# Two token groups through both layers of a two-layer decoder trunk, the second group's first mixer spread over the first group's whole way

## The chip, the cores and the metric

The kernel is one program on one NeuronCore of a Trainium2 chip. Its metric is the device time of one execution in microseconds (us), the median of three runs. The core has five engines with their own instruction streams: TensorE (PE, matrix products; its weight loads are shown as PEld), VectorE (DVE), ScalarE (ACT), GpSimd (POOL) and SyncE (SP), which here issues nearly all DMA transfers. They wait for one another by semaphores. Each engine carries out its instructions in the order in which they were written, so an instruction that waits holds up all that stand behind it on its engine. Matmuls accumulate in PSUM, eight banks of 512 float32 per partition; all else is in SBUF or in HBM, the chip's main memory.

## What is computed

One step of a decoder with two layers and a model width of 1024, for 1024 prompt tokens and 8 x 8 sample tokens, 1088 columns in all:

```python
for layer in range(2):
    hn = rms_norm(h, norm_mix_g[layer])
    if layer == 0:     # conformer convolution beside stick-breaking attention
        a_val, a_gate, q, k, v = split(hn @ w_in_even)              # 5 x 512
        a = silu(layer_norm(causal_conv31(a_val * sigmoid(a_gate))))
        b = stick_breaking_attention(q, k, v)   # sample tokens: paged past K and V too
        mix = concat(a, b) @ w_out_even
    else:              # short gated convolution beside causal pooling
        gb, gc, xv, u = split(hn @ w_in_odd)                        # 4 x 512
        c = gb * causal_conv3(gc * xv)
        d = per_group_linear(trailing_mean(u) - u) * pool_scale     # windows 2, 4, 8, 16
        mix = concat(c, d) @ w_out_odd
    h = h + mix
    g, u = split(rms_norm(h, norm_ffn_g[layer]) @ w_ffn_in[layer])  # 2 x 2816
    h = h + (silu(g) * u) @ w_ffn_out[layer]
y = rms_norm(h, norm_final_g)
```

Everything is float32. New keys, values and convolution and pooling states are returned beside `y`.

## The kernel before

Activations lie transposed, channels on the partitions and tokens in the columns: `hb` holds the residual in 8 chunks of 128 channels by 1088 columns. A float32 product is made of three: weights and activations are each split into a high part and a rest (`hl` and `x1`), and `mm3` adds high x high, high x rest and rest x high. A weight tile of 512 KB (8 slices of 128 x 128) is loaded by SP into `stage`, copied by ScalarE (L152) and subtracted by GpSimd (L153) into `hl`. Both have three buffers; `w_next` hands out one tile and starts the split two ahead. The order of the tiles is the list `seq`.

Columns are worked in groups. `GA` is the first 512 prompt tokens, one matmul of 512 columns per slice and product. `GB` is the other 512 and the 64 sample tokens, two matmuls of 288. `GT` is all 1088, in 364, 364 and 360. Weights of layer 0 are therefore read and split twice, those of layer 1 once.

The stages in order: input projection of A (0 to 157 us), of B (to 349.6), output projection and channel mixer of A (to 1096.6), the same of B (to 1576.9), then layer 1 for all columns (to 2656), and the last output blocks with the final norm.

`run_in` makes an input projection of 128 output channels per tile; its first two tiles run slice by slice together (`pair`), so that the norm of the input (`norm_hooks`) can be made meanwhile. `run_out` makes an output projection, which begins and ends with a pair. `run_ffn` makes the channel mixer: for every two of its 22 hidden chunks four input tiles (`one`), then the output blocks of the two chunks before (`out_block`, six matmuls of A each, evicted by `added`, L230). A chunk's product and its split into `hid` are put on the list `post` and written when `flush` is next called. Every matrix result is evicted by VectorE, scaled (L226) or added (L230). `prep` makes a next operand, high part on ScalarE (L304), rest on VectorE (L307). `mix_operand` splits a mixer's result into `x1` and reloads the residual from `park` in HBM.

Work with little matrix content runs between the matmuls as a generator. `bg` writes its next piece; `slot` is a place where that is called, after every two slices of a tile, after each tile and each output block. While A does its output projection and channel mixer of layer 0, the flow is: attention of B (scores L801, sigmoids L806, scans L815 and L818, product L820, transposes L830, values L839), then the convolution of B (L693) with the attention of the sample tokens (page transposes L928, scores L951, weight transposes L1000, values L1012), then the norm after the convolution. `drain` writes what is left at once.

In layer 1 `ev_u` and `ev_xv` evict, and put on `post` the window sums (`f2`, then `f3` with the pooling matmuls, L1348) and the gated product on GpSimd with the short convolution (L1271, L1281, L1292). At the end `to_y` works the last output blocks in 24 items of 384 columns or fewer, transposes each (L1402), multiplies by the gain and, per 384 tokens, scales by the norm and stores.

Of the kernel before, what the change touches and what calls it, by code (L numbers as in the profile page):

```python
# [16 lines left out]
D = 1024  # L17
# [29 lines left out]
GT = Grp(0, T, 364)  # L47
# [11 lines left out]
def trunk_kernel(ctx, tc, x_prompt, x_sample, cache_k, cache_v, state_conformer, state_shortconv, state_pool,  # L59
# [14 lines left out]
    tmpbox = [gstack.enter_context(tc.tile_pool(name="tmpg", bufs=4, side="right")), 640]  # L74

    def tmp():
        return tmpbox[0].tile([128, tmpbox[1]], F, name="tmp")
# [42 lines left out]
    for _ in range(2):  # L120
        for j, c in EVEN:
            add_in(w_in_even[0], 512 * j + c * 128)
    for _ in range(2):
        for n in range(8):
            add_in(w_out_even[0], n * 128)
        add_ffn(0)

    ODD = [(j, c) for c in range(4) for j in (3, 1, 2, 0)]
# [104 lines left out]

    def flush():
        todo = post[:]
        post.clear()
        for f in todo:
            f()
# [41 lines left out]
    def run_in(g, accs, x, evacs, hooks, ks=K0, tail=(lambda: None,) * 2):  # L280
        a0, a1 = pair(g, accs, x, K0, hooks)
        evacs[0](a0)
        evacs[1](a1)
        for i, e in enumerate(evacs[2:]):
            h = w_next()
            a = accs()
            end = i == len(evacs) - 3
            block(g, a, h, x, ks if end else K0, flush)
# [3 lines left out]
            if end:  # L292
                tail[1]()
        flush()
# [57 lines left out]
    def run_ffn(g, accs, ps, hidp, x, last, sig=False, slot=lambda: None):  # L352
# [16 lines left out]
        def ev_u(f, a):  # L369
# [7 lines left out]
            def fin():  # L377
                pool.tensor_tensor(t[:, :n], t[:, :n], u[:, :n], op=OP.mult)  # L378
                split(dst, t[:, :n])
# [10 lines left out]
        for q in range(G + 1):  # L390
            if q < G:
                for f in (2 * q, 2 * q + 1):
                    if f == 0:
                        run_in(g, accs, x, [ev_g, lambda a: ev_u(0, a)], norm_hooks(g, ps))
# [4 lines left out]
            if q == G:  # L399
                flush()  # L400
# [214 lines left out]
    def ev_k(g, hp):  # L615
        def f(a):
            scaled(g, kall[:, hp, g.cs], a)
            post.append(lambda: rows_out(g, kall[:, hp, g.cs], k_p, k_s, hp))
        return f

    def ev_v(g, hp):
        def f(a):
            t = tmp()
            scaled(g, t[:, :g.n], a)
            post.append(lambda: rows_out(g, t, v_p, v_s, hp))
# [130 lines left out]
    def attention(g):  # L756
# [3 lines left out]
        with ExitStack() as es_:  # L760
# [11 lines left out]
            def operands(h):  # L772
# [7 lines left out]
                for c in range(0, NKEY, 512):  # L780
                    small.append(lambda c=c: dve.tensor_tensor(k[o, c:c + 512], ks[:, c:c + 512],
                                                               f32(k[r, c:c + 512]), op=OP.subtract))
                small.append(lambda: act.activation(q[o], qs, AF.Copy))
                small.append(lambda: dve.tensor_tensor(qz[hh][r], qs, f32(q[r]), op=OP.subtract))
# [297 lines left out]
    def in_proj(g, x, first, slot):  # L1082
# [21 lines left out]
        flush()  # L1104

# [44 lines left out]

    acc_pool(GA, 3)
    hstack = ExitStack()
    hidp = hstack.enter_context(tc.tile_pool(name="hid0", bufs=2, side="right"))
# [39 lines left out]
    hstack.close()  # L1193


    acc_pool(GB, 3)
    run_out(GB, accs, x1, FFNG)
    tstack, r1stack = ExitStack(), ExitStack()
    sq = list(range(KC))

    def slot_d():
        turn[0] += 1
        if sq and turn[0] % 4 == 0:
            n = sq.pop(0)
            add_squares(GA, hb[:, n, GA.cs], n == 0)

    def to_mixer(hh):
        nonlocal x1
        assert not sq
        x1stack.close()  # L1210
        gstack.close()
        tmpbox[:] = [tstack.enter_context(tc.tile_pool(name="tmps", bufs=3, side="right")), 1152]
        r1p = r1stack.enter_context(tc.tile_pool(name="r1", bufs=1, side="right"))
        x1 = [r1p.tile([128, 2, T], FR, name=f"x1t_{c}") for c in range(KC)]
        for o in range(2):
            h = w_next()
            for i in range(4):
# [257 lines left out]
```

## Time and profile before

| | us |
|---|---|
| median of 3 runs (2706.16 to 2709.74) | 2708.54 |
| the profiled execution's own time | 2708.54 |
| its span, first to last instruction | 2706.8 |
| TensorE busy | 2603.3 |
| VectorE busy | 1212.3 |
| GpSimd busy | 1031.1 |
| ScalarE busy | 868.3 |

In a row of the timeline stand start, duration, engine, line, operation, tile written and read, shape and count, and in brackets the idle time of the engine before it with what ended it. In a row of groups the count is followed by busy time, mean ns of one, and idle time before them. In a row of windows stand the window, its length, the busy time of PE, PEld, DVE, ACT and POOL, the granted TensorE clock, the busy share of the DMA engines and GB/s. Matmuls overlap; their rate is read from start to start.

### The profile page before, as it was taken

How to read it: one execution, taken by the hardware profiler on the slowest of the kernel's cores; microseconds unless marked ns; L12 is line 12 of the kernel's file. 1: busy time of each engine (PE TensorE's matmuls, PEld its weight loads, DVE VectorE, ACT ScalarE, POOL GpSimd, SP SyncE). 2: the span in 40 equal slices, each digit the busy share in tenths (PEclk: the TensorE clock that was granted, in tenths of full speed). 3: DMA queues.
4: the chain of work that ended last, by engine and by line, in shares of the span. 5: the costliest groups of instructions: out<-in, count | busy, mean ns of one | idle time of the engine just before them, and what ended most of it. 6: DMA issues, size and time to landing. Idle time of an engine off the chain costs nothing. (4 is left out here: it accounts for less than half of the span.)

```text
span 2706.8 us, 37823 instructions
## 1 busy us (share of the span) xinstructions
PE 2603.3 (96%) x15423; PEld 2365.3 (87%) x15423; DVE 1212.3 (45%) x1730; ACT 868.3 (32%) x1326; POOL 1031.1 (38%) x589
## 2 busy tenths in 40 slices
PE   8989998998999998999999989999999999999997
PEld 6788876887666656899999989999999999999997
DVE  4774776868677642322222243343122222222226
ACT  4436765653433323332222232132211111111112
POOL 5655243343333337464444442224222222222222
PEclk9999999999999999999999999999999999999999
DMA  6432231234444432422222221131111111111111
GB/s 198 123 96 78 66 99 40 62 90 133 144 137 146 120 110 70 136 86 86 79 86 87 79 91 47 43 106 47 39 48 39 47 47 40 48 47 40 47 39 67
DMA packets 293380, 218.75 MB, mean 81 GB/s; under 512 B 21505, under 2 KB 248961, under 8 KB 293192
## 3 DMA queue, kind: packets, MB, share of 16 engines
q1 hardware_dynamic: 293176, 216.33, 26.8%
q8 instruction: 122, 2.00, 0.3%
q14 instruction: 50, 0.41, 0.1%
q10 hardware_dynamic: 32, 0.01, 0.0%
HBM read 198.09 MB, written 18.69 MB: 80 GB/s over the span
## 5 line engine op out<-in xcount | busy, mean ns | idle before, releaser
L153 POOL TENSOR_TENSOR hl<-stage,hl 128x1024 fp32r<-128x1024 f32 x278 | 679.5, 2446 | 1209.9 <-ACT hl L152 816.6
L170 PE MATMUL acc<-x1t,hl 128*128 128x364 f32 (+1 forms) x4896 | 824.1, 330 | 7.1 <-DVE hb L230 6.5
L170 PEld LDWEIGHTS acc<-x1t,hl 128*128 128x128 f32 x4896 | 817.2, 189 | 9.2 <-ACT x1t L304 6.7
L170 PE MATMUL acc<-x,hl 128*128 128x288 f32 (+1 forms) x4704 | 804.3, 325 | 12.9 <-DVE hb L230 9.6
L170 PEld LDWEIGHTS acc<-x,hl 128*128 128x128 f32 x4704 | 690.8, 189 | 88.7 <-issue 39.6
L170 PE MATMUL acc<-hid,hl 128*128 128x364 f32 (+2 forms) x3024 | 530.4, 333 | 20.5 <-DVE hb L230 17.5
L170 PEld LDWEIGHTS acc<-hid,hl 128*128 128x128 f32 x3024 | 480.0, 190 | 58.4 <-DVE hb L230 23.2
L152 ACT ACTIVATE hl<-stage 128x1024 fp32r<-128x1024 f32 x278 | 292.1, 1054 | 585.9 <-PE acc L170 318.5
L226 DVE TENSOR_TENSOR tmp<-acc,rr 128x728 f32<-128x728 f32 (+2 forms) x230 | 160.6, 720 | 684.3 <-PE acc L170 681.6
L230 DVE TENSOR_TENSOR hb<-acc,hb 128x728 f32<-128x728 f32 (+2 forms) x368 | 255.3, 720 | 273.2 <-PE acc L170 272.2
L176 DVE TENSOR_TENSOR hid<-tmp,hid 128x512 fp32r<-128x512 f32 (+2 forms) x66 | 60.8, 921 | 201.8 <-ACT hid L175 201.6
L187 POOL TENSOR_TENSOR ss<-ss,tmp 128x512 f32<-128x512 f32 (+2 forms) x55 | 98.4, 1789 | 91.6 <-ACT tmp L186 89.3
L378 POOL TENSOR_TENSOR tmp<-tmp 128x512 f32<-128x512 f32 (+2 forms) x66 | 117.1, 1774 | 29.3 <-ACT tmp L366 28.2
L175 ACT ACTIVATE hid<-tmp 128x512 fp32r<-128x512 f32 (+2 forms) x66 | 53.4, 809 | 230.8 <-POOL tmp L378 230.8
L170 PE MATMUL acc<-x1a,hl 128*128 128x512 f32 x480 | 122.4, 408 | 3.7 <-POOL hl L153 2.3
L366 ACT ACTIVATE tmp<-tmp 128x576 f32<-128x576 f32 (+1 forms) x44 | 39.6, 900 | 256.1 <-DVE tmp L226 256.1
L170 PEld LDWEIGHTS acc<-x1a,hl 128*128 128x128 f32 x480 | 89.9, 191 | 27.1 <-POOL hl L153 3.8
L693 DVE SCALAR_TENSOR_TENSOR cacc<-ext,par,cacc 128x512 f32<-128x512 f32 x120 | 90.1, 751 | 2.3
L364 POOL TENSOR_TENSOR tmp<-tmp 128x512 f32<-128x512 f32 x22 | 31.7, 1439 | 120.3 <-ACT tmp L363 113.1
L839 PE MATMUL o<-wt,vrow 128*64 128x128 f32 x576 | 76.6, 278 | 0.4 <-ACT wt L831 0.4
L818 DVE TENSOR_TENSOR_SCAN q<-q,ones 128x384 f32<-128x384 f32 (+6 forms) x56 | 76.0, 1357 | 2.0
L655 DVE SCALAR_TENSOR_TENSOR cacc<-ext,par,cacc 128x512 f32<-128x512 f32 x100 | 75.4, 754 | 3.0
(222 smaller groups left out, 1880.2 us busy)
## 6 DMA issues: line engine op xcount, KB each, us to landing
stage<-in_w_ffn_in_dram SPq DMA_DIRECT2D x132, 512.0 KB
stage<-in_w_ffn_out_dram SPq DMA_DIRECT2D x66, 512.0 KB
stage<-in_w_in_even_dram SPq DMA_DIRECT2D x40, 512.0 KB
kst<-in_cache_k_dram SPq DMA_DIRECT2D x64, 256.0 KB
vst<-in_cache_v_dram SPq DMA_DIRECT2D x64, 256.0 KB
stage<-in_w_out_even_dram SPq DMA_DIRECT2D x16, 512.0 KB
stage<-in_w_in_odd_dram SPq DMA_DIRECT2D x16, 512.0 KB
park<-hb SPq DMA_DIRECT2D x16, 288.0 KB
```

Source lines behind the costliest of these rows:

```text
L152: act.activation(hl[:, 0], st, AF.Copy)
L153: pool.tensor_tensor(hl[:, 1], st, f32(hl[:, 0]), op=OP.subtract)
L170: pe.matmul(acc[:, b, :c1 - c0], w, x[:, xi, c0:c1], start=first and s == 0, stop=last and s == 2)
L176: dve.tensor_tensor(dst[:, 1], src, f32(dst[:, 0]), op=OP.subtract)
L187: pool.tensor_tensor(ss[:, g.cs], ss[:, g.cs], t[:, :g.n], op=OP.add)
L226: dve.tensor_tensor(d, a, r, op=OP.mult)
L230: dve.tensor_tensor(d, a, d, op=OP.add)
L378: pool.tensor_tensor(t[:, :n], t[:, :n], u[:, :n], op=OP.mult)
L655: dve.scalar_tensor_tensor(acc, i, w, acc, op0=OP.mult, op1=OP.add)
L693: dve.scalar_tensor_tensor(o, i, w, o, op0=OP.mult, op1=OP.add)
L818: dve.tensor_tensor_scan(e, e, ones[:, 0:1].to_broadcast([128, n - 128]), q[:, n - 128:n - 127], op0=OP.mult, op1=OP.mult)
L839: pe.matmul(o, vrow[h][:, j], w[:, j], start=j == 0, stop=j == i)
```

## The change

There is no group of all columns any more. A goes through layer 0 and layer 1 to its last residual; then B does. The weights of layer 1 are read and split once for each. The flow of B's layer 0 mixer is the same, but is called in every second slot (`bg2`) of A's way from the first output projection to the last channel mixer, whose slots now include those of `run_in`. A's layer 1 hands the last 15 pooling inputs and the last 2 convolution inputs to B (`uhalo`, `ghalo`). The first 512 rows of `y` are made and stored by a new flow, `flow_y`, in slots of B's output projection and channel mixer of layer 0; the end works 16 items, of 256 and 320 columns.

Smaller edits: the rest of a hidden chunk's split goes on a second list, `late`, written one `flush` later; the row copies of keys and values (`rows_out`) are written one `flush` later; the rests of the attention's keys and queries are subtracted by GpSimd instead of VectorE. `tmp` keeps 4 buffers of 640 columns throughout, where layer 1 had 3 of 1152.

```diff
     for _ in range(2):
         for n in range(8):
             add_in(w_out_even[0], n * 128)
         add_ffn(0)
-    for j, c in ODD:
-        add_in(w_in_odd[0], j * 512 + c * 128)
-    for n in range(8):
-        add_in(w_out_odd[0], n * 128)
-    add_ffn(1)
+        for j, c in ODD:
+            add_in(w_in_odd[0], j * 512 + c * 128)
+        for n in range(8):
+            add_in(w_out_odd[0], n * 128)
+        add_ffn(1)
...
+    late = []
+
     def flush():
-        todo = post[:]
+        todo, low_parts = post[:], late[:]
         post.clear()
-        for f in todo:
+        late.clear()
+        for f in todo + low_parts:
             f()
...
-    def run_in(g, accs, x, evacs, hooks, ks=K0, tail=(lambda: None,) * 2):
-        a0, a1 = pair(g, accs, x, K0, hooks)
+    def run_in(g, accs, x, evacs, hooks, ks=K0, tail=(lambda: None,) * 2, slot=lambda: None):
+        a0, a1 = pair(g, accs, x, K0, hooks, slot)
...
             def fin():
                 pool.tensor_tensor(t[:, :n], t[:, :n], u[:, :n], op=OP.mult)
-                split(dst, t[:, :n])
+                act.activation(dst[:, 0], t[:, :n], AF.Copy)
+                late.append(lambda: dve.tensor_tensor(dst[:, 1], t[:, :n], f32(dst[:, 0]), op=OP.subtract))
...
             if q == G:
+                flush()
                 flush()
                 last(hid.pop(q - 1))
...
-            post.append(lambda: rows_out(g, kall[:, hp, g.cs], k_p, k_s, hp))
+            post.append(lambda: post.append(lambda: rows_out(g, kall[:, hp, g.cs], k_p, k_s, hp)))
...
-                    small.append(lambda c=c: dve.tensor_tensor(k[o, c:c + 512], ks[:, c:c + 512],
-                                                               f32(k[r, c:c + 512]), op=OP.subtract))
+                    small.append(lambda c=c: pool.tensor_tensor(k[o, c:c + 512], ks[:, c:c + 512],
+                                                                f32(k[r, c:c + 512]), op=OP.subtract))
...
+    def to_mixer(g, slot):
+        def f(hh):
+            for o in range(2):
+                h = w_next()
+                for i in range(4):
+                    n = o * 4 + i
+                    a = accs()
+                    out_block(g, a, h, i, hh)
+                    added(g, hb[:, n, g.cs], a)
+                    sp.dma_start(park[:, n, g.cs], hb[:, n, g.cs])
+                    prep(g, x1, n, pc(MIXG + 8 + n), squares=True)
+                    low(1)
+                    slot()
+            low()
+        return f
+
+    def mixer1(g, slot):
+        own = g is GA
...
+                    def f2():
+                        pool.tensor_tensor(q[:, :g.n], q[:, :g.n], t[:, :g.n], op=OP.mult)
+                        ext = mx.tile([128, 2 + NX], F, name="ext1")
+                        act.activation(ext[:, 2:514], q[:, 0:512], AF.Copy)
...
+                        if own:
+                            pool.memset(ext[:, 0:2], 0.0)
+                            act.activation(ghalo[:, c], q[:, 510:512], AF.Copy)
+                        else:
...
+                            pe.transpose(m[:66, 0:128], q[:, 510:576], ident)
+                            act.activation(rowc[:66, c * 128:c * 128 + 128], m[:66, 0:128], AF.Copy)
...
+            evs = [(ev_gb, ev_gc, ev_xv, ev_u)[j](c) for j, c in ODD]
+            run_in(g, accs, x1, evs, norm_hooks(g, ms), ks=KS, slot=slot,
+                   tail=(lambda: mix_operand(g, x1, KS[:1]), lambda: mix_operand(g, x1, KS[1:7])))
+            mix_operand(g, x1, KS[-1:])
...
+    turn[0] = 0
+
+    def bg2():
+        turn[0] += 1
+        if turn[0] % 2:
+            bg()
+
     mix_operand(GA, x1, K0)
-
-    run_out(GA, accs, x1, FFNG, slot=bg)
+    run_out(GA, accs, x1, FFNG, slot=bg2)
+    ffn(GA, to_mixer(GA, bg2), True, bg2)
+    mixer1(GA, bg2)
+    run_out(GA, accs, x1, FFNG + 8, KS, slot=bg2)
 
     def last_a(hh):
         drain()
...
                 out_block(GA, a, h, i, hh)
                 mix_operand(GB, x1, [n])
                 added(GA, hb[:, n, GA.cs], a)
-                sp.dma_start(park[:, n, GA.cs], hb[:, n, GA.cs])
-
-    run_ffn(GA, accs, ms, hidp, x1, last_a, sig=True, slot=bg)
+                add_squares(GA, hb[:, n, GA.cs], n == 0)
+
+    ffn(GA, last_a, True, bg2)
 
     acc_pool(GB, 3)
-    run_out(GB, accs, x1, FFNG)
...
+    def flow_y():
+        with tc.tile_pool(name="ya", bufs=1) as yp:
...
+            norm_cols(ms, D, 0, 4)
+            yield 1
+            for n in range(8):
+                m = ms()
+                for t in range(4):
+                    pe.transpose(m[:, t * 128:t * 128 + 128], hb[:, n, t * 128:t * 128 + 128], ident)
+                dve.tensor_tensor(y[:, :, n * 128:n * 128 + 128], m.rearrange("p (t c) -> p t c", t=4),
+                                  gall[:, None, n * 128:n * 128 + 128].to_broadcast([128, 4, 128]), op=OP.mult)
+                yield 1
+            for t in range(4):
+                act.activation(y[:, t], y[:, t], AF.Copy, scale=rstd[:, t:t + 1])
+                sp.dma_start(y_p[0, t * 128:t * 128 + 128], y[:, t])
+                yield 1
+
+    flow.append(flow_y())
+    run_out(GB, accs, x1, FFNG, slot=bg2)
+    ffn(GB, to_mixer(GB, lambda: None), False, bg2)
+    drain()
+    mixer1(GB, lambda: None)
+    run_out(GB, accs, x1, FFNG + 8, KS)
...
+    YB = ((0, 256), (256, 576))
...
-        for q in range(24 + LAG):
-            if q < 24:
+        for q in range(16 + LAG):
+            if q < 16:
                 item(q)
...
+    ffn(GB, to_y, False, lambda: None)
```

More of the change, by code (lines that the diff above doesn't have):

```diff
@@ L122, in trunk_kernel @@
             add_in(w_in_even[0], 512 * j + c * 128)
+    ODD = [(j, c) for c in range(4) for j in (3, 1, 2, 0)]
     for _ in range(2):
@@ L287, in run_in @@
             end = i == len(evacs) - 3
-            block(g, a, h, x, ks if end else K0, flush)
+            block(g, a, h, x, ks if end else K0, flush, slot)
             if end:
@@ L1104, in in_proj @@
         flush()
+        flush()
     phase = {}
```

353 lines of the change are left out of this document (164 added, 189 removed).

## The prediction

> **What bounds the kernel now.** I read the page first, then busy time by stage, then TensorE's waits, then the timeline at the longest of them.
>
> ```profile
> span 2706.8 us, 37823 instructions
> PE 2603.3 (96%) x15423; PEld 2365.3 (87%) x15423; DVE 1212.3 (45%) x1730; ACT 868.3 (32%) x1326; POOL 1031.1 (38%) x589
> ```
>
> The span is 2706.8 us, and TensorE is without work for 2706.8 - 2603.3 = 103.5 us of it. The profiled execution's own time is 2708.54 us, 1.74 us above its span; it is also the median of the three runs. By stage (length, TensorE's busy time, the other engines', the granted clock):
>
> ```profile
> 0.00:157.00 157.00, 138.97 (x611) 107.44 (x612) 97.91 (x149) 73.31 (x106) 94.92 (x63) 0.99 0.52 153
> 157.00:349.60 192.60, 184.73 (x1323) 170.69 (x1321) 116.84 (x171) 111.89 (x224) 86.97 (x82) 0.98 0.27 76
> 349.60:1096.60 747.00, 694.60 (x3257) 512.64 (x3257) 505.83 (x736) 334.35 (x589) 291.16 (x180) 0.97 0.36 108
> 1096.60:1576.90 480.30, 472.04 (x3567) 470.66 (x3567) 142.09 (x184) 135.31 (x161) 237.78 (x115) 1.00 0.30 89
> 1576.90:2656.00 1079.10, 1077.12 (x6436) 1070.09 (x6436) 315.80 (x408) 195.86 (x217) 302.87 (x133) 1.00 0.16 48
> 2656.00:2706.80 50.80, 35.84 (x235) 33.75 (x234) 33.84 (x85) 17.59 (x31) 17.35 (x18) 0.90 0.24 89
> ```
>
> Layer 1 (1576.9 to 2656) is idle for 2.0 us in 1079: only its matmuls count there. Half of all idle time, 747.0 - 694.6 = 52.4 us, lies where group A does layer 0's output projection and channel mixer with the flow of group B's mixer between its matmuls. TensorE's waits in that stretch (total, times, longest):
>
> ```profile
> PE acc L170 <- DVE hb L230: 26.9, 8, 7.4
> PE m L1000 <- ACT wts L1001: 9.5, 4, 3.7
> PE m L830 <- DVE be L820: 7.5, 5, 3.5
> ```
>
> **The matmuls themselves.** Layer 1 has 16 + 8 + 44 + 22 = 90 weight tiles of 24 (slice, product) steps each. A step was three matmuls of 364, 364 and 360 columns; it becomes one of 512 in A and two of 288 in B.
>
> ```profile
> 1042.51 15.64 PE L170 MATMUL acc<-x,hl 128*128 128x512 f32 x66
> 1057.98 0.40 PE L170 MATMUL acc<-hid,hl 128*128 128x512 f32 x1
> ...
> 1215.80 24.49 PE L170 MATMUL acc<-x,hl 128*128 128x288 f32 x184
> ...
> 2007.99 42.32 PE L170 MATMUL acc<-x1t,hl 128*128 128x364 f32 x253
> ```
>
> (1057.98 - 1042.51)/66 = 234.4 ns, 24.49/184 = 133.1 ns, 42.32/253 = 167.3 ns. Old step 501.9 ns, new 234.4 + 266.2 = 500.6 ns: 2160 x -1.3 = **-3 us**. So two passes over layer 1 cost TensorE nothing.
>
> The splits of a weight tile, by the groups of instructions:
>
> ```profile
> L153 POOL TENSOR_TENSOR hl<-stage,hl 128x1024 fp32r<-128x1024 f32 x278 | 679.5, 2446 | 1209.9 <-ACT hl L152 816.6
> L152 ACT ACTIVATE hl<-stage 128x1024 fp32r<-128x1024 f32 x278 | 292.1, 1054 | 585.9 <-PE acc L170 318.5
> ```
>
> The 90 further weight tiles are 90 x (1.05 us on ScalarE and 2.45 us on GpSimd), under the 5.6 us that A's 24 matmuls take per tile.
>
> **What half the rate removes.** A piece of flow went into every turn, now into every second. By the code the flow has 73 + 180 + 31 = 284 pieces (attention, sample with convolution, norm), so it needs 567 turns; group A now has 31 + 256 + 8 + 63 + 31 + 256 = 645, and the flow ends inside its second channel mixer. VectorE, busy 505.8 of 747 us, gets about (747 + 2160 x 0.234)/747 = 1.7 times the time for the same pieces. Of the 26.9 us, 7.4 is one stop at 446 us and 9.5 lies in A's last output blocks (both below); the other 10 with 9.5 + 7.5 make 27 us of waits on the flow. I leave 8 (6 of them L1000's, whose nine transposes stand in one piece with two PSUM buffers, so its wait is its own): **-19**; bounds -27 and -5. The fill's deferred low part (`late`) belongs here: VectorE no longer stands before it.
>
> Long waits also cost clock (windows again, the third figure from the end):
>
> ```profile
> 446.00:449.00 3.00, 3.00 (x7) 2.36 (x8) 2.29 (x3) 2.98 (x5) 2.41 (x2) 0.50 0.56 163
> 1576.90:1580.00 3.10, 3.10 (x10) 3.10 (x11) 2.94 (x2) 1.70 (x2) 2.94 (x3) 0.50 1.03 374
> ```
>
> After the waits that end at 445.9 and 1576.9 us the granted clock is 0.50. The stretch's mean of 0.97 is 22 us of withheld clock in 747, about half of it while matmuls ran: 11 us, of which I take **-6** with the waits. [...]
>
> **The stop at 446 us**, in the timeline:
>
> ```profile
> 439.41 5.09 POOL L153 TENSOR_TENSOR hl<-stage,hl 128x1024 fp32r<-128x1024 f32 x2 [0.86 <-ACT hl L152]
> 439.50 5.55 DVE L781 TENSOR_TENSOR kt<-kall,kt 64x512 fp32r<-64x512 f32 x2
> ...
> 445.91 1.19 PE L170 MATMUL acc<-x,hl 128*128 128x512 f32 x2 [7.38 <-DVE hb L230]
> ```
>
> From the output projection's closing pair to the channel mixer's opening pair, three weight buffers allow one prefetch, so the second tile is split only after the closing pair: 1.05 + 2.45 = 3.5 us whatever else happens. The rest was VectorE, held by two key subtractions (L781) ahead of the evictions; these go to GpSimd. 7.4 becomes about 3.9: **-3.5** (bounds -4 and 0). The same transition comes once more, in layer 1: **+4.5** with its clock. [...]
>
> **Group A's last blocks** (1058 to 1096.6). The stretch by its windows:
>
> ```profile
> 1030.00:1096.60 66.60, 54.19 (x220) 41.38 (x218) 26.52 (x40) 26.51 (x35) 40.86 (x24) 0.94 0.35 108
> ```
>
> and, in the timeline,
>
> ```profile
> 1072.58 0.63 ACT L175 ACTIVATE hid<-tmp 128x512 fp32r<-128x512 f32 x1 [5.89 <-POOL tmp L378]
> 1073.24 0.69 DVE L176 TENSOR_TENSOR hid<-tmp,hid 128x512 fp32r<-128x512 f32 x1 [8.77 <-ACT hid L175]
> 1074.59 10.70 PE L170 MATMUL acc<-hid,hl 128*128 128x512 f32 x36 [5.68 <-DVE hb L230]
> ...
> 1096.59 3.67 PE L170 MATMUL acc<-x,hl 128*128 128x288 f32 x26 [2.23 <-DVE hb L230]
> ```
>
> TensorE idles 12.4 us here, 9.5 of them for L230 (5.7, 2.2 and two below 1). The evictions stood behind L176, which waited for ScalarE, which waited for GpSimd still at the flow's norm. With `late` and a flow that has ended, 5.7 and some 2 of the rest go; the new squares and their GpSimd sums give about 2.5 back: **-5** (bounds -10 and +3).
>
> **The passage into layer 1.** In the timeline:
>
> ```profile
> 1576.88 5.36 PE L170 MATMUL acc<-x1t,hl 128*128 128x364 f32 x20 [6.46 <-DVE hb L230]
> ```
>
> and VectorE's groups kept apart by shape, the first of the stretch 1555 to 1577, the others of the whole span:
>
> ```profile
> L307 DVE SCALAR_TENSOR_TENSOR x1t<-hb,par,x1t 128x1088 fp32r<-128x1088 f32 x7 | 13.3, 1906 | 0.3 <-ACT x1t L304 0.3
> ...
> L230 DVE TENSOR_TENSOR hb<-acc,hb 128x576 f32<-128x576 f32 x96 | 71.4, 755 | 78.8 <-PE acc L170 78.3
> L307 DVE SCALAR_TENSOR_TENSOR x<-hb,par,x 128x576 fp32r<-128x576 f32 x16 | 21.1, 1332 | 6.0 <-ACT x L304 6.0
> L230 DVE TENSOR_TENSOR hb<-acc,hb 128x512 f32<-128x512 f32 x96 | 64.7, 684 | 20.5 <-PE acc L170 20.3
> L307 DVE SCALAR_TENSOR_TENSOR x<-hb,par,x 128x512 fp32r<-128x512 f32 x8 | 9.5, 1204 | 4.9 <-ACT x L304 4.9
> ```
>
> VectorE took 0.76 + 1.91 us per output block of 12 x 0.133 = 1.6 us, and the new PSUM pool waited: 6.46, and 3.1 - 10 x 0.167 = 1.4 for the clock. Now B needs 0.76 + 1.33 = 2.1 against 1.6, eight times 0.5 less the slack of the accumulators: 3. **-5**. Group A pays newly: 0.68 + 1.20 = 1.9 against 6 x 0.234 = 1.4, so **+4**.
>
> **Layer 1's token mixer, in halves.** In the gate block GpSimd multiplies, and a transpose of the product stands in the middle of that block on TensorE (from the chain of waits):
>
> ```profile
> 1773.81 1.07 ACT hl L152
> 1774.88 0.07 issue
> 1774.95 2.41 POOL hl L153
> 1777.35 2.50 POOL tmp L1271
> ...
> 1779.91 0.30 PE m L1281
> ```
>
> The chain from the block's start (1773.8) to the transpose takes 6.1 us and fits just in half a block of 72 x 0.167 / 2 = 6.0 us. In B half a block is 24 x 0.133 = 3.2 us; the chain keeps its first 3.5 us and multiplies 576 columns.
>
> ```profile
> L578 POOL TENSOR_TENSOR hb<-tmp 128x576 f32<-128x576 f32 x4 | 5.8, 1460 | 6.0 <-ACT tmp L576 6.0
> ```
>
> 1.1 + 2.4 + 1.5 = 5.0 against 3.2: 1.7 us of stop, four times, **+7**, with the 2 us of old waits gone **+5** (bounds 0 and +10). A has no such transpose, but the pooling matmuls behind VectorE's window sums come 5.6 us later instead of 12: **+2.5**, and 2 for the reload of the residual and the last low part (bounds 0 and +12 together). B's second passage from pair to pair waits as its first did:
>
> ```profile
> 1150.45 2.77 PE L170 MATMUL acc<-x,hl 128*128 128x288 f32 x19 [1.53 <-POOL hl L153]
> ```
>
> **+1.5**; and the low part deferred past the last block is late by some 0.5 us in four places, **+2**. In the input projections the row copies leave one flush later: **-1.5**, since the long stop at their end stays (it waits for an eviction behind the convolution). The first rows' 32 transposes and their norm leave the end and go into B's layer 0; TensorE does both, **+1** for the switching. The end keeps its last eight items, hence its length from the last matmul; **+0.5**.
>
> **Sum**: -3 - 19 - 6 - 3.5 + 4.5 - 5 - 5 + 4 + 5 + 2.5 + 2 + 1.5 + 2 - 1.5 + 1 + 0.5 = -20. 2706.8 - 20 + 1.7 = **2688 us**.
>
> **The rivals.** *More is gained*: the halves hide their chains (GpSimd runs ahead, so the 7 us vanish) and A's new waits are 5 instead of 13: 2688 - 15 = 2673. For it: B's layer 0 had, in 480 us, next to no wait but the quoted 6.5 and 1.5; against it: 3.2 us is short of the chain by the rows.
>
> *Nothing is left*: the waits on the flow fall by a third only (-9, clock -2), since the pieces are as long as before, and A's layer 1 meets the sample's pieces with its own VectorE work (+20 instead of +13): -20 + 10 + 4 + 7 = +1, 2709. For it: L1000 waits inside its own piece.
>
> *Slower*: the waits belong to group A's width, not to the flow's rate: three accumulators of one bank hold 2.8 us of output blocks, and any longer VectorE queue stops TensorE. Then the 52.4 stay, and A's 506 us (2160 x 0.234) of layer 1 bring waits at the same 7%, 38 us, in place of the 13; the gains of 19, 6, 3.5 and 5 are gone: -20 + 33.5 + 25 = +38.5, 2747. For it: from 1030 to 1096.6, with hardly any flow left, A still waited 12.4 us; against it: their causes are named above and are removed. It decides from 33 us of new waits in A (13 + 20).
>
> *It does not do what it says*: were the flow not used up, the rest would run uncovered before A's last blocks; 567 turns against 645 speak against it.
>
> **How the numbers follow.** Forecast 0.53 (own range 2675 to 2700), more gained 0.17, nothing left 0.15, slower 0.13, not used up 0.02 (about 2720). From 2666 to 2722 leaves out most of the slower case and the edge of the gain. Some 0.2% (5.4 us) is what a measurement can tell from no change. Faster: nearly all of 0.53, 0.17, a little of 0.15, together 0.71; within 0.2%: 0.10; slower: 0.19.
>
> **What would show it.** Right: TensorE idle about 75 us in all; L830 and the L230 waits inside A's blocks nearly gone; a wait of about 1.7 us before B's transposes in the gate blocks; no 6.5 us wait between B's layers; waits on hl of 3 to 4 us at both of A's passages into a channel mixer. Wrong: waits of evictions throughout A's layer 1, a period per 512 columns above 234 ns, or TensorE waiting for GpSimd's splits tile after tile.

## The result and the profile after

The change makes the kernel slower. Its median is 2728.27 us (2725.49 to 2731.74) against 2707.72 us (2706.16 to 2709.74) for the kernel before, timed beside it: a ratio of 1.0075, 95% interval 1.0059 to 1.0091, where 2688 us had been forecast. The profiled execution has a span of 2726.6 us and a time of its own of 2728.42 us. In the code of after some lines have other numbers: a weight tile's matmuls are L169, its high part L151 (ScalarE) and its rest L152 (GpSimd), residual evictions L229, operand splits L174 (high part, ScalarE) and L175 (rest, VectorE), and a square of the residual L185 (ScalarE) with its sum L186 (GpSimd).

The head of its page:

```profile
span 2726.6 us, 38626 instructions
PE 2612.3 (96%) x15423; PEld 2275.0 (83%) x15423; DVE 1271.2 (47%) x1781; ACT 983.6 (36%) x1530; POOL 1335.8 (49%) x775
```

TensorE idles 2726.6 - 2612.3 = 114.3 us, 10.8 more than before, and its matmuls take 9.0 us more; 75 us of idle time had been forecast. Where it happens is seen by cutting both traces where the same weight tile is split: after the input projections, at A's last output blocks, and at the start of B. Windows of after (A's way, then its last blocks):

```profile
157.00:356.60 199.60, 187.65 (x1322) 173.08 (x1320) 115.64 (x155) 112.19 (x224) 106.92 (x98) 0.97 0.26 73
356.60:1591.80 1235.20, 1193.61 (x5402) 912.26 (x5403) 691.99 (x955) 484.68 (x786) 621.13 (x362) 0.98 0.35 104
1591.80:1639.60 47.80, 31.96 (x169) 26.95 (x168) 22.88 (x28) 15.34 (x23) 15.96 (x10) 0.82 0.33 101
```

The same two stretches of before, where A's way is layer 0 alone:

```profile
349.60:1081.10 731.50, 682.87 (x3209) 504.10 (x3210) 491.48 (x719) 326.58 (x578) 285.25 (x177) 0.97 0.36 105
1081.10:1110.90 29.80, 26.02 (x156) 22.84 (x156) 15.86 (x19) 9.01 (x13) 7.39 (x3) 1.00 0.60 203
```

A's way now holds its layer 1: 506 us of weight matmuls, and pooling matmuls and two norms, which the groups of that stretch give (3.4 us for the pooling, about half of 4.2 and 4.1 for the norms, together 7.5; the table takes 7):

```profile
L217 PE MATMUL m<-tmp,ones 128*128 128x512 f32 x8 | 4.2, 610 | 0.9 <-DVE tmp L208 0.9
L193 PE MATMUL m<-ones,ss 128*128 128x1 f32 x34 | 4.1, 242 | 0.6 <-DVE kth L938 0.6
L1311 PE MATMUL m<-pp,pwp 128*128 128x512 f32 x12 | 3.4, 393 | 0.0
```

| stretch | before, with A's layer 1 moved | after | difference | forecast |
|---|---|---|---|---|
| input projections | 349.6 | 356.6 | +7.0 | -1.5 |
| A's way to its last blocks | 731.5 + 506.3 + 7 = 1244.8 | 1235.2 | -9.6 | -20.2 |
| A's last blocks into B | 29.8 | 47.8 | **+18.0** | +0.7 |
| all of B after that | 1595.9 - 513.3 = 1082.6 | 1087.0 | +4.4 | +1 |
| sum | 2706.8 | 2726.6 | +19.8 | -20 |

(The last column puts each term of the forecast where it lies. Of its -5 for A's last blocks, 5.7 is a wait at 1074.6, which by these cuts counts in A's way.) Of the 40 us between forecast and result, 17 lie in one stretch of 48 us. Here is its middle, in the timeline of after:

```profile
1601.77 0.68 DVE L229 TENSOR_TENSOR hb<-acc,hb 128x512 f32<-128x512 f32 x1
...
1602.48 0.63 ACT L185 ACTIVATE tmp<-hb 128x512 f32<-128x512 f32 x1 [2.03 <-DVE hb L229]
...
1603.02 0.67 ACT L174 ACTIVATE x<-hb 128x576 fp32r<-128x576 f32 x1
...
1603.72 1.44 DVE L175 TENSOR_TENSOR x<-hb,x 128x576 fp32r<-128x576 f32 x1 [1.27 <-ACT x L174]
1605.08 0.68 DVE L229 TENSOR_TENSOR hb<-acc,hb 128x512 f32<-128x512 f32 x1
1605.79 0.63 ACT L185 ACTIVATE tmp<-hb 128x512 f32<-128x512 f32 x1 [2.10 <-DVE hb L229]
...
1605.81 1.67 PE L169 MATMUL acc<-hid,hl 128*128 128x512 f32 x6 [1.64 <-DVE hb L229]
...
1607.97 2.78 DVE L175 TENSOR_TENSOR x<-hb,x 128x576 fp32r<-128x576 f32 x1 [2.22 <-ACT x L174]
...
1611.41 2.93 PE L169 MATMUL acc<-hid,hl 128*128 128x512 f32 x6 [3.93 <-DVE hb L229]
```

The brackets close a ring. The eviction (L229) releases the new square on ScalarE (L185); behind the square, in ScalarE's order, stands the high part of B's operand (L174); that releases its rest on VectorE (L175); and behind the rest stands the next eviction. One turn, from start to start of these four, is 0.71 + 0.54 + 0.70 + 1.36 = 3.31 us (1601.77 to 1605.08), where TensorE's six matmuls take 6 x 0.234 = 1.4. No engine of the ring is busy throughout (in this turn VectorE 1.44 + 0.68 us, ScalarE 0.63 + 0.67): it is a sum of latencies. Its end:

```profile
1621.56 5.69 PE L169 MATMUL acc<-x,hl 128*128 128x288 f32 x24 [7.23 <-DVE hb L229]
```

And the stretch by windows (third figure from the end: granted clock) also shows half clock, 0.53 over 18 us:

```profile
1609.00:1627.00 18.00, 8.37 (x30) 7.29 (x31) 8.43 (x8) 6.47 (x9) 8.55 (x6) 0.53 0.33 96
```

TensorE's waits in A's way (in total, times, longest):

```profile
PE acc L169 <- DVE hb L229: 17.1, 9, 9.1
PE m L1006 <- ACT wts L1007: 6.7, 4, 2.8
PE m L934 <- DVE kth L938: 5.4, 2, 2.8
PE acc L169 <- DVE x L175: 4.0, 1, 4.0
PE acc L169 <- POOL hl L152: 3.0, 2, 1.7
```

The longest, at the passage into A's channel mixer, in the timeline:

```profile
414.26 1.42 DVE L311 SCALAR_TENSOR_TENSOR x<-hb,par,x 128x512 fp32r<-128x512 f32 x2 [1.37 <-ACT x L308]
...
418.89 3.40 POOL L787 TENSOR_TENSOR kt<-kall,kt 64x512 fp32r<-64x512 f32 x2
...
419.37 6.22 DVE L311 SCALAR_TENSOR_TENSOR x<-hb,par,x 128x512 fp32r<-128x512 f32 x3
...
422.60 5.19 POOL L152 TENSOR_TENSOR hl<-stage,hl 128x1024 fp32r<-128x1024 f32 x2 [0.30 <-POOL kt L787]
...
425.52 2.56 DVE L821 TENSOR_TENSOR_SCAN q<-q,ident 128x128 f32<-128x128 f32 x1
...
431.04 1.28 DVE L229 TENSOR_TENSOR hb<-acc,hb 128x512 f32<-128x512 f32 x2
...
431.87 3.69 PE L169 MATMUL acc<-x,hl 128*128 128x512 f32 x8 [9.10 <-DVE hb L229]
```

The key subtractions stand on GpSimd now (L787), but VectorE is not free for the evictions. Its operand rests (L311) take 6.22 / 3 = 2.07 us beside the key subtractions and the weight split, where 1.42 / 2 = 0.71 was enough five microseconds earlier, and the 128-column scan (L821) takes 2.56 beside the weight split; the stop is 9.1 us, not 3.9.

### The profile page after: what moved, and what is told of

Its sections match the earlier page's. It is cut to its first block, busy times and chain, and to the rows that moved or that the text cites. A ratio compares the mean times of both kernels' runs of the same rounds, so it can differ in the third digit from the quotient of the medians.

```text
span 2726.6 us, 38626 instructions
## 1 busy us (share of the span) xinstructions
PE 2612.3 (96%) x15423; PEld 2275.0 (83%) x15423; DVE 1271.2 (47%) x1781; ACT 983.6 (36%) x1530; POOL 1335.8 (49%) x775
## 5 line engine op out<-in xcount | busy, mean ns | idle before, releaser
L169 PE MATMUL acc<-x,hl 128*128 128x288 f32 (+1 forms) x9600 | 1646.7, 329 | 34.1 <-DVE hb L229 19.9
L169 PEld LDWEIGHTS acc<-x,hl 128*128 128x128 f32 x9600 | 1444.0, 190 | 192.4 <-issue 51.5
L152 POOL TENSOR_TENSOR hl<-stage,hl 128x1024 fp32r<-128x1024 f32 x368 | 896.2, 2438 | 965.7 <-ACT hl L151 707.2
L169 PE MATMUL acc<-hid,hl 128*128 128x288 f32 (+1 forms) x3072 | 539.1, 332 | 15.4 <-DVE hb L229 14.4
L151 ACT ACTIVATE hl<-stage 128x1024 fp32r<-128x1024 f32 x368 | 386.1, 1053 | 444.6 <-PE acc L169 226.1
L169 PEld LDWEIGHTS acc<-hid,hl 128*128 128x128 f32 x3072 | 465.0, 189 | 75.8 <-DVE hb L229 22.4
L225 DVE TENSOR_TENSOR tmp<-acc,rr 128x512 f32<-128x512 f32 (+1 forms) x230 | 166.4, 724 | 754.9 <-PE acc L169 752.9
L229 DVE TENSOR_TENSOR hb<-acc,hb 128x512 f32<-128x512 f32 (+1 forms) x376 | 269.6, 722 | 282.3 <-PE acc L169 281.3
L186 POOL TENSOR_TENSOR ss<-ss,tmp 128x512 f32<-128x512 f32 (+1 forms) x69 | 101.0, 1463 | 131.1 <-ACT tmp L185 130.2
L382 POOL TENSOR_TENSOR tmp<-tmp 128x512 f32<-128x512 f32 (+1 forms) x88 | 120.5, 1369 | 17.7 <-ACT tmp L370 17.4
L169 PE MATMUL acc<-x1a,hl 128*128 128x512 f32 x480 | 122.5, 409 | 3.6 <-POOL hl L152 2.3
L169 PEld LDWEIGHTS acc<-x1a,hl 128*128 128x128 f32 x480 | 90.4, 192 | 27.0 <-POOL hl L152 3.8
L699 DVE SCALAR_TENSOR_TENSOR cacc<-ext,par,cacc 128x512 f32<-128x512 f32 x120 | 90.1, 751 | 2.3
L311 DVE SCALAR_TENSOR_TENSOR x<-hb,par,x 128x576 fp32r<-128x576 f32 (+1 forms) x56 | 75.1, 1357 | 22.4 <-ACT x L308 22.4
L185 ACT ACTIVATE tmp<-hb 128x512 f32<-128x512 f32 (+1 forms) x69 | 44.6, 647 | 96.0 <-DVE hb L229 86.0
```

The lines of the kernel that those rows point to most:

```text
L151: act.activation(hl[:, 0], st, AF.Copy)
L152: pool.tensor_tensor(hl[:, 1], st, f32(hl[:, 0]), op=OP.subtract)
L169: pe.matmul(acc[:, b, :c1 - c0], w, x[:, xi, c0:c1], start=first and s == 0, stop=last and s == 2)
L186: pool.tensor_tensor(ss[:, g.cs], ss[:, g.cs], t[:, :g.n], op=OP.add)
L225: dve.tensor_tensor(d, a, r, op=OP.mult)
L229: dve.tensor_tensor(d, a, d, op=OP.add)
```

## The experiments

Each was timed beside the kernel before on the same chip, and ratios are to that kernel. The differences from after in the text are of medians as they stand, though the kernel before took some 2 us less beside after than here. If each kernel is first set against the kernel before of its own timing, the first four edits come to 16.2, 11.6, 10.6 and 22.2 us where the text has 14.4, 9.7, 12.5 and 24.0; so these figures hold to about 2 us.

| kernel | median us | before us | ratio (95%) |
|---|---|---|---|
| after, squares of A later | 2713.91 | 2709.59 | 1.0016 (1.0006 to 1.0026) |
| after, rests on VectorE | 2718.58 | 2709.59 | 1.0035 (1.0024 to 1.0046) |
| after, flow in every turn | 2740.73 | 2709.59 | 1.0115 (1.0098 to 1.0132) |
| after, no `late` | 2752.28 | 2709.51 | 1.0161 (1.0144 to 1.0178) |
| after, squares and rests repaired | 2702.04 | 2709.51 | 0.9983 (0.9973 to 0.9994) |
| the same, row transposes later | 2697.67 | 2709.51 | 0.9957 (0.9941 to 0.9974) |
| that one, four weight buffers | 2707.47 | 2709.51 | 0.9994 (0.9985 to 1.0004) |
| squares, rests and row transposes as above, row copies as before | 2700.64 | 2709.13 | 0.9968 (0.9957 to 0.9980) |
| before, squares in A's last blocks | 2724.66 | 2709.59 | 1.0057 (1.0040 to 1.0074) |
| before, rests on GpSimd | 2719.54 | 2709.13 | 1.0035 (1.0023 to 1.0048) |
| before, with `late` | 2696.19 | 2709.13 | 0.9950 (0.9934 to 0.9967) |
| before, with `late` and row copies later | 2695.50 | 2708.20 | 0.9952 (0.9938 to 0.9966) |

**The squares.** Taken out of A's last blocks and put into the first pieces of the flow beside B:

```diff
                 added(GA, hb[:, n, GA.cs], a)
-                add_squares(GA, hb[:, n, GA.cs], n == 0)
...
-            yield 1
+            for n in range(KC):
+                add_squares(GA, hb[:, n, GA.cs], n == 0)
+                yield 1
+            for _ in range(4):
+                yield 1
             norm_cols(ms, D, 0, 4)
```

> The changed kernel with the squares of group A's last residual taken out of its last output blocks and made in the first eight pieces of the flow of the first rows. Theory 1 (a ring over three engines: in each of A's last blocks the square on ScalarE waits for the eviction, the next block's operand copy stands behind the square, its rest on VectorE waits for the copy, and the next eviction stands behind the rest; 3.3 us a block where TensorE needs 1.4): the passage from A's last blocks into B falls from the 27 us that it takes now to about 12, 16 to 20 us less in all, 2710 us. Theory 2 (the blocks are slow because GpSimd is busy and holds VectorE's two-input instructions): the eight GpSimd sums only move, VectorE's rests stay at 1.4 us, and no more than 5 us are gained, 2723 us or more.

And the same instruction put into the kernel before, alone:

```diff
                 sp.dma_start(park[:, n, GA.cs], hb[:, n, GA.cs])
+                add_squares(GA, hb[:, n, GA.cs], n == 0)
...
-    sq = list(range(KC))
+    sq = []
```

> The kernel before with one thing of the change: the squares of A's residual are made in A's last output blocks (of layer 0) instead of in slots of B's channel mixer. Theory 1 (the ring): A's last eight blocks grow from about 14 us to about 26, 10 to 18 us slower, 2718 to 2725 us. Theory 2 (GpSimd's load): here too GpSimd has the eight sums, but fewer of its own, so 5 us at most, 2713 us.

Out of after: 2728.27 to 2713.91, 14.4 us less, a little under the 16 to 20 expected. Into before: 2709.59 to 2724.66, 15.1 us more, as expected. The stretch's window of the kernel with the squares moved:

```profile
1591.40:1621.80 30.40, 26.85 (x160) 23.35 (x159) 16.39 (x20) 11.09 (x17) 10.25 (x6) 1.00 0.49 159
```

and of the kernel before with the squares added:

```profile
1080.10:1126.90 46.80, 30.73 (x157) 26.11 (x156) 20.14 (x19) 13.86 (x22) 15.96 (x10) 0.82 0.43 129
```

30.4 and 46.8 us, beside 47.8 of after and 29.8 of before: eight ScalarE squares with their GpSimd sums decide it, with two groups or without. In before with the squares the ring turns as in after: three evictions start at 1086.84, 1090.09 and 1093.39 us. The edit moves squares and sums together, so the share of each is read from the trace only: VectorE's rest waits for ScalarE in every turn (1.27 us in the brackets), and the sums lengthen it by about 0.7 us (last section). With both gone, VectorE's evictions follow each other at TensorE's pace again, as the timeline of after with the squares moved shows (1604.75 - 1603.49 = 1.26 us):

```profile
1603.49 0.68 DVE L229 TENSOR_TENSOR hb<-acc,hb 128x512 f32<-128x512 f32 x1
1604.09 0.74 DVE L175 TENSOR_TENSOR x<-hb,x 128x576 fp32r<-128x576 f32 x1
...
1604.75 0.68 DVE L229 TENSOR_TENSOR hb<-acc,hb 128x512 f32<-128x512 f32 x1
```

**The rests of keys and queries.** Back on VectorE in after:

```diff
-    pool.tensor_tensor(k[o, c:c + 512], ks[:, c:c + 512], ...
+    dve.tensor_tensor(k[o, c:c + 512], ks[:, c:c + 512], ...
...
-    pool.tensor_tensor(qz[hh][r], qs, f32(q[r]), op=OP.subtract)
+    dve.tensor_tensor(qz[hh][r], qs, f32(q[r]), op=OP.subtract)
```

> The changed kernel with the rests of the attention's keys and queries subtracted by VectorE again, as before the change. Theory 1 (on GpSimd they come late behind the weight splits and lengthen VectorE's instructions beside them): B's input projection, 7 us longer than before the change, gets 4 to 6 us back, and the stop ahead of A's first channel mixer (9.1 us) falls to 7 or less: 2718 to 2723 us. Theory 2 (they help VectorE, and the 7 us come from the row copies that are written one flush later): no gain, or 3 to 10 us slower, 2728 to 2738 us.

The opposite edit in the kernel before:

> The kernel before with one edit alone: the rests of keys and queries are subtracted by GpSimd. Theory 1 (they come late on GpSimd and slow the weight splits and VectorE's instructions beside them): 4 to 10 us slower, ratio 1.0015 to 1.0037, with group B's input projection 3 to 7 us longer and the stop before A's channel mixer no shorter than 7 us. Theory 2 (the forecast's: the subtractions leave VectorE's way): 2 to 4 us faster, the stop at 446 us about 4 us.

Again both ways agree: 9.7 us gained in after, 10.4 lost in before. Most of it lies before A's output projection, in B's input projection, where the attention's first pieces run: A's output projection begins at 350.1 us instead of 356.6, and in the kernel before at 355.4 instead of 349.6. TensorE's waits there (157 to 360 us) in after:

```profile
PE z L807 <- POOL kt L787: 4.7, 1, 4.7
PE m L836 <- DVE be L826: 3.7, 6, 0.8
```

and with the rests on VectorE:

```profile
PE z L807 <- ACT crow L594: 2.9, 1, 2.9
PE m L836 <- DVE be L826: 1.1, 2, 0.9
```

What theory 1 expected of the stop failed in both kernels. In after, where 7 us or less was expected, giving the rests back to VectorE left the stop at 8.25 us: at half the rate another piece, with two scans and a product, stands ahead of the evictions. In the kernel before, where the order of the pieces had not moved and no less than 7 us was expected, the stop of 7.4 shrank to 1.69 and, a few us on, a wait for the weight split:

```profile
455.28 1.22 PE L170 MATMUL acc<-x,hl 128*128 128x512 f32 x2 [3.74 <-POOL hl L153]
```

So the forecast's 3.5 us of split were there. But A's output projection had begun 5.8 us later, so the edit as a whole lost.

**The rate of the flow.** Two groups, a piece in every turn:

```diff
     def bg2():
         turn[0] += 1
-        if turn[0] % 2:
+        if every[0] or turn[0] % 2:
             bg()
```

(`every` is cleared before the flow of the first rows.)

> The changed kernel with group B's flow called in every turn of group A's way instead of every second; it then ends inside A's first channel mixer, and A's layer 1 runs alone. Theory 1 (the waits on the flow depend on its rate; at half the rate they fell from some 34 us to 21): 8 to 15 us slower, 2736 to 2743 us, with the waits on the scans and in the output blocks back. Theory 2 (the waits belong to the pieces and to A's width; the half rate only spreads them and brings them into layer 1): within 5 us of 2728, or faster by what A's layer 1 waits for the flow now, 5 to 8 us.

12.5 us more than after: half the rate is worth about that much within the two groups. But the waits that were expected back in the output blocks did not come. Over A's way TensorE waited for evictions 2.5 us where after waited 17.1. The norms (L217, 0.9 in after), the scans (L836, 4.6 for 1.2) and the splits (7.8 for 3.0) waited longer instead:

```profile
PE m L217 <- DVE tmp L208: 8.2, 2, 5.7
PE acc L169 <- DVE hb L229: 2.5, 3, 1.7
```

A's way is 9 us longer than in after (1244.4 for 1235.2), 5 of it idle time of TensorE; B, whose code is the same, took another 4, which stays unexplained.

**`late`.** Taken out of after:

```diff
-                act.activation(dst[:, 0], t[:, :n], AF.Copy)
-                late.append(lambda: dve.tensor_tensor(dst[:, 1], t[:, :n], f32(dst[:, 0]), op=OP.subtract))
+                split(dst, t[:, :n])
```

> The changed kernel with the rest of a hidden chunk's split written at once again, without the second list. Prediction's reading (VectorE no longer stands before a rest that waits for ScalarE and GpSimd; this was worth some 10 us of waits in A's blocks): 5 to 12 us slower, 2733 to 2740 us, with waits for evictions back in A's output blocks. Rival (the waits came from the rate of the flow alone): within 3 us of 2728.

24 us more than after, twice what was expected. TensorE's waits on evictions in A's way are 32.0 us instead of 17.1:

```profile
PE acc L169 <- DVE hb L229: 32.0, 15, 9.1
```

Then the same edit alone in the kernel before, which has no second group in layer 1 and the flow at full rate:

> The kernel before with one edit alone: the rest of a hidden chunk is written one flush later (late). Theory 1: a VectorE that stands before the rest's ScalarE copy is what makes TensorE wait beside the flow, whatever the token groups; A's channel mixer of layer 0 loses about half of its 36 us of waits on VectorE and of the clock they cost: 12 to 20 us less than before, ratio 0.9925 to 0.9955. The two groups as such, without late, would then be what costs (2752 without late against 2708 before). Theory 2: late only repairs what the two groups add; in the kernel before it changes less than 4 us (0.9985 to 1.0015).

2709.13 to 2696.19, 12.9 us less, with some ten lines changed. The waits on evictions over A's way, in before:

```profile
PE acc L170 <- DVE hb L230: 23.1, 5, 7.4
```

and the waits there with `late`:

```profile
PE acc L170 <- DVE hb L230: 13.8, 3, 7.4
PE m L1005 <- ACT wts L1006: 8.9, 4, 3.1
PE m L835 <- DVE be L825: 3.5, 3, 2.0
```

The waits on evictions there fall from 23.1 us to 13.8: those at 1027 and 1074 us (4.4 and 5.7) are gone, as the forecast's reading of that place said. What remains is the stop of 7.4 and 6.5 us in two waits at 650 and 658 us. Some of it comes back in A's last blocks, in two waits of 1.3 and 1.0 us.

**The repaired two-group kernel.** Squares later and rests on VectorE together:

> The changed kernel with both: A's squares made later and the attention's rests on VectorE. Theory 1 (two separate costs, the ring of 14 us and GpSimd's rests of 10 us): they add up, 2728 - 14 - 10 = 2704 us, about 5 us below the kernel before. Rival (both free the same engine, GpSimd, so that the second brings less): 2709 to 2714 us.

2702.04, beside 2728.3 - 14.4 - 9.7 = 2704.2 by adding: the two losses are separate. To this, B's transposes of the gate product (L1238) written one flush after the product:

```diff
-                            m = ms()
-                            pe.transpose(m[:66, 0:128], q[:, 510:576], ident)
+                            def rows():
+                                m = ms()
+                                pe.transpose(m[:66, 0:128], q[:, 510:576], ident)
...
+                            post.append(rows)
```

> As the kernel with both, and in B's layer 1 the transposes of the last rows of the gated product are written one flush later than the product. The prediction's own mechanism (TensorE stands 1.3 to 1.65 us, four times, before these transposes, for GpSimd's product): the four waits vanish, 6 us less than with both alone, 2698 us. Rival (the product's late arrival is only handed on, to the convolution and the eviction of the gate): the wait moves to the next consumer, no gain.

2697.67, 4.4 us less (the two intervals just touch). The wait that goes is this one, in TensorE's waits of after over B's layer 1 (2100 to 2300):

```profile
PE m L1238 <- POOL tmp L1222: 6.3, 4, 1.7
```

The forecast had 7 us for these four. Some of the gain comes back: one wait of 1.7 us on L175 appears at 2198.7.

Then a fourth weight buffer, paid for with one of the three staging buffers, and splits three tiles ahead:

```diff
-hl = wpool.tile([128, 2, 1024], FR, name="hl", bufs=3)
+hl = wpool.tile([128, 2, 1024], FR, name="hl", bufs=4)
...
-name="stage", bufs=3
+name="stage", bufs=2
```

> As the kernel with the rows later, and with four buffers of split weights and a split three tiles ahead (the staging buffers go from three to two, for room). Theory 1 (at each passage from a closing pair to an opening pair TensorE waits for the second tile's split, 1.5 us in B and 3 to 8 us in A): these waits vanish in all four places, 8 to 12 us less, 2688 us. Rival (A's stop before its channel mixer, 8.2 us, is VectorE's queue alone, and two staging buffers make the loads late): at most 3 us less or slower.

The waits on splits fall from 8.4 us to 2.3 in the whole span:

```profile
PE acc L169 <- POOL hl L152: 2.3, 2, 1.2
```

The stop before A's channel mixer stays at 8.2, so it was VectorE's queue and not the weights; and the kernel as a whole is 9.8 us slower: A's input projection alone ends 7 us later. The missing staging buffer may be the reason; no run tests it apart. The row copies of keys and values, in the kernel with three weight buffers, put back to where the kernel before the change has them:

```diff
-post.append(lambda: post.append(lambda: rows_out(...)))
+post.append(lambda: rows_out(...))
```

> The best kernel so far (squares later, rests on VectorE, row transposes one flush later; 2697.7 us) with the row copies of keys and values written at the flush at which the kernel before writes them. Theory 1 (the forecast's term): leaving one flush later is worth 1.5 us, so this one takes 1 to 3 us more, ratio 0.9961 to 0.9968. Theory 2: it makes no difference, 0.995 to 0.996.

2700.64, 3.0 us more, but the intervals of the two overlap. In the profiles 1.9 us of it lie in A's input projection (its end 156.4 for 154.5), and that end was at 156.5 too in after with the rests on VectorE, where the row copies are late. In the kernel before with `late`, leaving the row copies one flush later was timed too:

> The kernel before with the two edits that the runs so far show as gains, and without the two token groups: late, and the row copies one flush later. Theory 1: the two add up (13 us and about 2 us), 2693 to 2695 us, ratio 0.9937 to 0.9945, at or below the best two-group kernel's 0.9957; then none of the gains needs the two groups. Theory 2: the row copies gain only in the two-group kernel, where they leave beside a slower flow: 2696 us, 0.995, no better than late alone.

2695.50 beside 2696.19, within the intervals of both. So what the row copies are worth stays open between 0 and 3 us. The three best kernels, this one, `late` alone and the repaired two-group kernel with its transposes later, do not differ within their intervals (0.9952, 0.9950, 0.9957).

## Why the prediction was wrong

**What failed first: group A's last blocks, -5, measured +18.** The step said that the new squares "give about 2.5 back", without working that out, and its upper bound was +3. It removed the waits that it saw: the 5.7 us went, as the runs with `late` show, while the one of 2.2 stayed (2.1 with `late` alone). It did not ask in whose order the square stands. A square stands before the operand copy for which VectorE waits, and VectorE's next instruction is the eviction for which the square waits. Two in-order engines that wait for each other twice per block took 3.3 us for a block of 1.4. The order stood in the diff. Some of the 18 us is clock: in the window of 18 us the granted clock was 0.53, and over the whole stretch TensorE was busy 31.96 us, 26.85 with the squares elsewhere. With the squares elsewhere the stretch took 30.4 us, as before the change.

**The subtractions on GpSimd: -3.5 at the stop, measured +1.7, and 6.5 us in B's input projection for which there was no term.** (The stop was 7.38 us and is 9.10. The input projections were to gain 1.5 by the row copies and lost 7.0; with the rests back on VectorE they lost 0.5.) The forecast saw what VectorE loses and not what stands behind on GpSimd: the weight split, and at B's first attention piece the scores themselves (4.7 us of wait, 3.2 before). The two L781 that it read took 5.55 / 2 = 2.8 us each, beside weight splits on GpSimd, where the median of all 24 in the kernel before is 0.69; and that contention moved along: in the rows above L311 takes 2.07 us beside the key subtractions and the weight split on GpSimd, and 0.71 without.

**Waits on the flow, -19, and clock, -6.** In A's way TensorE's idle time went from 731.5 - 682.9 = 48.6 to 1235.2 - 1193.6 = 41.6 us, 7 less where the terms of that stretch make 14. The waits there by L229 without the stop, by L1006 and by L934 are still 8.0 + 6.7 + 5.4 = 20 us, where 8 had been left. Those by the attention's transposes did nearly go, as said (7.5 to 1.2). Spreading pieces in time did not shorten the waits inside a piece: L934 and L1006 wait for the evictions of their own transposes, and only L1006 was named for that. And the rate was not what kept evictions waiting: with `late` and the flow at full rate they waited 2.5 us in A's way. The clock was hardly given back: TensorE's own time fell by 2.6 us (1193.6 beside 682.9 + 506.3 + 7), not 6, and the forecast's "about half of it" was worked out from no row. After some of the new waits the granted clock is 0.50, as after the old ones. This window of after follows a wait of 2.62 us by L934, up to which TensorE had been busy:

```profile
1008.80:1012.20 3.40, 3.40 (x10) 2.81 (x11) 1.95 (x3) 1.38 (x3) 2.37 (x1) 0.50 0.00 0
```

and this one a wait of 1.83 by L1006:

```profile
872.30:875.70 3.40, 3.24 (x16) 2.54 (x16) 2.14 (x4) 2.03 (x4) 0.80 (x1) 1.00 0.00 0
```

The length of a wait alone does not decide it in these traces: after one of 2.35 us in before (to 704.8) the clock stayed at 1.00 (704.8 to 708.2), and after one of 2.17 in after (to 829.9) it was 0.50 from 831.3 to 834.7.

**`late`, folded into those 19, was the gain.** The forecast named it in one clause and gave the credit to the rate. The runs price them apart: `late` 24 us within two groups and 12.9 without, half the rate some 11 to 12.5 within two groups. The kernel before with `late` (2696.2) and the repaired two-group kernel (2697.7) do not differ. So the two groups as such gain nothing measurable in these versions. That what their slower flow saves is given back by the waits in A's layer 1, the second passages and the losses in B fits the waits listed, but no run takes it apart.

**What held.** Two passes over layer 1's weights cost TensorE next to nothing; in the best two-group kernel its busy time is 2.1 us above before's 2603.3:

```profile
PE 2605.4 (97%) x15423; PEld 2271.2 (84%) x15423; DVE 1281.4 (48%) x1821; ACT 983.9 (36%) x1530; POOL 1283.1 (48%) x735
```

The flow ended inside A's second channel mixer, as its turns had been counted: its norm runs from 1360 to 1450 us, and A's last blocks come after 1590. B's transposes waited 6.3 us for 7: four times 1.3 to 1.65. The passage into B's layer 1 lost its 6.5 us wait; 1.83 is left:

```profile
2109.38 0.91 PE L169 MATMUL acc<-x,hl 128*128 128x288 f32 x5 [1.83 <-DVE hb L229]
```

B's second passage waited 1.51 for 1.5. A's new places waited 7.9 us where their terms make 10.5: 1.5 for evictions at its passage into layer 1 (4), 4.0 at L175 before its second output projection (2), and 0.7 + 1.7 for a split at its second passage into a channel mixer (4.5 with its clock). The 1 us for switching between matmuls and transposes is shown by no run: in after, four transposes of the first rows stretch 24 matmuls of B from 24 x 0.133 = 3.19 us to 3.64 (1642.00 to 1645.64), but what part of the 0.45 is switching the trace does not tell.

**The rivals.** The *slower* one had the sign and not the reason: it asked for evictions late throughout A's layer 1, with 33 us of new waits. From 946 to 1591.8 us, A's layer 1, evictions kept TensorE waiting 2.6 us in all, and from 1250 on, in its channel mixer, TensorE is busy 340.75 of 341.8 us:

```profile
1250.00:1591.80 341.80, 340.75 (x1422) 256.00 (x1421) 125.08 (x191) 98.56 (x137) 198.77 (x107) 1.00 0.33 99
```

The width of A is no limit by itself. *More is gained* needed B's four waits to vanish, and they came. *Nothing is left* came nearest in its reason (pieces as long as before), but it had neither of the two edits that cost 24 us.

## What to carry to other kernels

When an instruction is added to a helper engine inside a loop, write down the cycle that it closes: if A waits for B's last instruction and B's next one stands behind something that waits for A, the loop's period is the sum of their latencies, however idle the engines are (here 3.31 us a turn, in which VectorE was busy 2.12 us and ScalarE 1.30). Before crediting a large restructuring with a gain, price its small edits alone in the old structure: here ten lines of it gave 12.9 us, two other edits cost 24, and the restructuring itself gave nothing that could be measured. Moving an instruction to a less busy engine moves it ahead of something there; ask what that is, and whether the two engines slow each other (here a rest of 0.71 us took 2.07 beside GpSimd's instructions).

## What the hardware showed unexpectedly

Contention of GpSimd and VectorE is larger than the forecast allowed, and of the rows read here the shortest instruction was lengthened most: the scan of 128 columns took 0.42 us alone and 2.56 beside a weight split (L821 at 415.59 and 425.52 in after), the 128x512 rest 0.71 and 2.07, and the 128x576 rest in A's last blocks 0.74 us with the squares gone, 1.44 beside the squares' GpSimd sums and 2.78 beside a weight split. By the difference, 1.44 - 0.74 = 0.7, an estimated 0.7 of the ring's 3.3 us is contention, not order. The long scan began at 425.52, the two weight splits beside it ended at 422.60 + 5.19 = 427.79, and the scan at 428.08, 0.29 us after them. The first of the scan's rows, in the timeline of after:

```profile
415.59 0.42 DVE L821 TENSOR_TENSOR_SCAN q<-q,ident 128x128 f32<-128x128 f32 x1
```
